# Value products of two attentions and a state-space mixer: values as the stationary operand, output by feature

## The chip, the cores and the metric

One core of one Trainium2 chip runs the whole kernel. The metric is device time in microseconds (us) of one execution; lower is better. The engines are TensorE (PE in the profile; PEld is its loading of the stationary operand), VectorE (DVE), ScalarE (ACT), GpSimd (POOL) and SyncE (SP, which issues the large loads).

## What is computed

One layer of a hybrid encoder, in float32: 256 tokens behind 16 meta tokens (272 in all), width 2048. The normed input is projected with `w_in`; four mixers of 512 features each work on the projection; their outputs are joined, projected with `w_out`, and a gated feed-forward block follows. Three mixers matter here. FoX and DSA are attentions of eight heads of 64 features; FoX with forget gates and a causal mask, DSA with keys chosen by an index score:

```python
s = jnp.where(key_pos[None, :] <= qpos[:, None], s, -jnp.inf)      # FoX
p = jax.nn.softmax(s, axis=-1).astype(v.dtype)
return jnp.einsum('bhqk,bkhd->bqhd', p, v)
```

SSD is a state-space mixer, also eight heads of 64 features. The kernel computes it as one masked product over all earlier tokens, `y = sum over s of m[l, s] * xdt[s] + d * x`, where `m` holds the decays times the products of the two projections `b` and `c`, and `xdt` is the input times its step `dt`.

## The kernel before, in words

**Weights.** All weights stream once from memory as 1 MB tiles (128 partitions x 2048). Each half tile is split into two parts of a shorter type, `whi` on ACT (line 148) and `wlo` on DVE (line 154), with four buffers of each. `tile_matmuls` (line 186) then issues, for each 128x128 block, three matmuls: high weights with high activations (line 202), high with low (203), low with high (204). In the projection these move 258 or 272 columns of tokens; the weights are stationary.

**Order.** The mixers are generators. After each half tile of weights (24 matmuls) `step(2)` (line 165) advances up to two of them to their next `yield`. So a mixer's work lies between half tiles of the projection. The instructions' final order on each engine is made by the framework's planner, which keeps dependences and goes by its own estimate of durations; on the chip each engine then runs its queue strictly in that order.

**Attention** (line 493, used by DSA and FoX) works on two tiles of 128 queries, `qt` 1 with 144 keys and `qt` 2 with 272. Scores come by query (lines 505 and 508), the maximum on DVE (513), the exponentials on ACT with their sum `st` (516). DVE then takes the reciprocal of the sums (518) and copies the meta tokens' part into `sm` (520). PE turns `sm` (522) and the eight heads' scores (531) to get the probabilities by key, copied by ACT to `p0` (524) and `pt` (533). For the values, `pt[:, h, :]` is stationary (128 keys x 128 queries) and the 64 columns of `v` of that head move (539); the meta tokens of all heads are one product of `p0` with a block-diagonal `blk` of 512 columns (541). The output `po` is by query; DVE multiplies it with the reciprocals into `o` (543); PE turns `o` back by feature with four transposes (547); ACT and DVE take its high and low parts `mh` and `ml` (549, 550), which `w_out` needs by feature. A float32 matmul shows as two records in the trace (two passes), a transpose as one.

**SSD** (line 672) keeps decays times products in `e1` (8 heads x 256 queries) and `e2` (8 x 128). `e1` is loaded by a DMA from POOL's queue (line 690) into the buffer that FoX's bias held, then DVE (699), ACT (700) and DVE (728) work on it. For `qt` 0, 1, 2 (2, 128 and 128 tokens) the values are formed as in the attention: `e1`, `e2` stationary, 64 columns of `xdt` moving (738, 741), the meta tokens' `e0` with `blk` of 512 columns (742), a copy on ACT (744), four transposes (748), and on DVE the skip term (750), four instructions per tile, into `yt`. The gate, the norm and the parts for `w_out` follow (757 to 769).

**Output projection.** For each group of four feature tiles of `w_out` the mixers come in the order DSA, pool, FoX, SSD; `drain(name)` first issues what is left of a mixer.

Of the kernel before, what the change touches and what calls it, by code (L numbers as in the profile page):

```python
# [12 lines left out]
P = 128  # L13
# [8 lines left out]
H = 8  # L22
# [15 lines left out]
# token tiles of all tokens (the meta tokens, then two of 128) and of the tokens whose mixed value is used  # L38
# [3 lines left out]
# per-partition columns  # L42
# [7 lines left out]
# constants: the unit matrix, its upper triangle, and rows that matmuls spread over the partitions  # L50
# [3 lines left out]
# groups of four feature tiles of w_in, by first column of the reference's order  # L54
# [15 lines left out]
# rows of w_out by the order in which the mixers end: dsa, fox, ssd, pool  # L70
# [9 lines left out]
def hybrid_layer(ctx: ExitStack, tc, t):  # L80
# [57 lines left out]
    def split_hi(i, half, n, pool=None):  # L138
        """The first parts of half a weight tile, in n pieces; gives the steps to the second parts."""
        load(i)  # L140
        hi = (pool or wpool).tile([P, 1024], F32R, tag="whi", bufs=4, name="whi")
        lo = (pool or wpool).tile([P, 1024], F32R, tag="wlo", bufs=4, name="wlo")
        halves[i, half] = (hi, lo)
        steps = []
        for q in range(n):
            c = slice(1024 * q // n, 1024 * (q + 1) // n)
            src = raws[i][:, 1024 * half + c.start:1024 * half + c.stop]
            act(hi[:, c], src, AF.Copy)  # L148
            steps.append((lo[:, c], src, hi[:, c].bitcast(F32)))
        return iter(steps)  # L150
# [35 lines left out]
    def tile_matmuls(accs, hi_lo, kts, n, feat, first, last, sub=None):  # L186
        """accs[f] += W tile.T @ activations; feat: weights stationary."""
        i = state["next"]
        state["next"] += 1
        for half in range(2):  # L190
            if (i, half) not in halves:
                split(i, half)
        load(i + 1)
        load(i + 2)
        def pair(f, half, kk):
            hi, lo = halves[i, half]
            k = 2 * half + kk
            xh, xl = hi_lo(kts[k])
            c = slice(kk * 512 + f * P, kk * 512 + (f + 1) * P)
            st = first and k == 0  # L200
            en = last and k == 3
            mm(accs[f][:, :n], hi[:, c], xh, start=st, stop=False)  # L202
            mm(accs[f][:, :n], hi[:, c], xl, start=False, stop=False)  # L203
            mm(accs[f][:, :n], lo[:, c], xh, start=False, stop=en)  # L204

        for part in range(2):
            if (i + 1, part) not in halves:
                split(i + 1, part)
            if last:
                # feature tile by feature tile, so that they end one after the other  # L210
                for f in (2 * part, 2 * part + 1):
                    for k in range(4):
                        pair(f, k // 2, k % 2)
            else:
                # the last feature tile's bank may still be read when a group begins
                late = first and part == 0 and i > 0
                for f, kk in sorted(((f, kk) for f in range(4) for kk in range(2)),
                                    key=lambda c: (c[0] == 3, c[1], c[0]) if late else (c[1], c[0])):
                    pair(f, part, kk)
            step(STEPS)  # L220
        for half in range(2):
            del halves[i, half]

# [1 line left out]
    def rstd_columns(small, sq, scale, segs, ps, meanwhile=None):  # L225
        """sq: lists of [128, tokens] whose sum over partitions and entries is the sum of squares."""
# [17 lines left out]
    def rsqrt(v, s, y, z, meanwhile=None):  # L244
        """y = v ** -0.5: a square root, a reciprocal and a step of Newton's method."""
# [11 lines left out]
    def rstd_rows(small, sq, scale, segs, out_rows):  # L257
        """The same by token along the free axis, on every partition."""
# [13 lines left out]
    # ================= input, mixers =================  # L272
# [19 lines left out]
    def root_table():  # L292
        """Loads the table of the square root before an argument waits for it."""
        pin(act(root, ones[:, 0:1], AF.Sqrt))
# [3 lines left out]
    def keep_warm(n):  # L298
        """Keeps TensorE's clock up while it waits."""
        ps = mix_ps()  # L300
        for _ in range(n):
            mm(ps[:, 0:P], ones, ones, start=True, stop=True)
# [82 lines left out]
    def small_values():  # L385
# [29 lines left out]
        # x: softplus; val: dt * -exp(a_log) and log_sigmoid  # L415
# [35 lines left out]
        # by head: the last two meta tokens' forget gates for FoX, the meta tokens' sums and dt for SSD  # L451
# [31 lines left out]
    def repeat(src, n, name):  # L483
        """The meta tokens once for each head, along the free axis."""
# [8 lines left out]
    def attention(name, q, k, v, blk, bias):  # L493
        """q, k by feature, v by token; bias(tile): the biases per head and the tile for the scores."""
        mh, ml = mixed_out(name)
        for qt, nk in ((1, 144), (2, 272)):
# [21 lines left out]
            V.reciprocal(st[:, 2, :], st[:, 1, :])  # L518
            sm = M.tile([P, P], F32, tag="p0", bufs=2, name="sm")
# [6 lines left out]
            for kt in range(1, qt + 1):  # L526
# [8 lines left out]
                pts.append(pt)  # L535
            po = mix_ps()
            for h in range(H):
                for j, pt in enumerate(pts):
                    mm(po[:, HD * h:HD * h + HD], pt[:, h, :], v[:, 1 + j, HD * h:HD * h + HD],
                       start=(h == 0 and j == 0), stop=False, skip_group_check=True)  # L540
            mm(po, p0, blk, start=False, stop=True, skip_group_check=True)
            o = M.tile([P, H, HD], F32, tag="o", bufs=2, name="o")
            V.tensor_tensor(o, po.rearrange("p (h d) -> p h d", d=HD), bcast(st[:, 2, :], [[1, H], [0, HD]]), ALU.mult)
            yield
            ps = mix_ps()
            for f in range(4):
                nc.tensor.transpose(ps[:, f * P:(f + 1) * P], o[:, 2 * f:2 * f + 2, :], ident)
            pv = ps.rearrange("p (a b) -> p a b", b=P)
# [3 lines left out]
        # the last two meta tokens, all heads at once: row 32 * pair + 2 * head in pair + token  # L552
# [119 lines left out]
    def ssd():  # L672
# [24 lines left out]
        # decays, from the sums of dt * a up to each token; later tokens' are masked with the scores  # L697
# [35 lines left out]
        for qt in (0, 1, 2):  # L733
            c0, n = SEGQ[qt]
            py = mix_ps()
            for h in range(H if qt else 0):
                hs = slice(HD * h, HD * h + HD)
                mm(py[:, hs], e1[:, h, (qt - 1) * P:qt * P], xdt[:, 1, hs], start=(h == 0), stop=False,
                   skip_group_check=True)
                if qt == 2:  # L740
                    mm(py[:, hs], e2[:, h, :], xdt[:, 2, hs], start=False, stop=False, skip_group_check=True)
            mm(py[0:n, :], e0[:, c0:c0 + n], blk, start=(qt == 0), stop=True, skip_group_check=True)
            y = M.tile([P, 512], F32, tag="o", bufs=2, name="y")
            act(y[0:n, :], py[0:n, :], AF.Copy)
            yield
            ps = mix_ps()
            for f in range(4):
                nc.tensor.transpose(ps[:, f * P:f * P + n], y[0:n, f * P:(f + 1) * P], ident[0:n, 0:n])
            for f in range(4):
                V.scalar_tensor_tensor(yt[:, f, c0:c0 + n], xs[:, f, L - LQ + c0:L - LQ + c0 + n], col(C_DSKIP + f),  # L750
                                       ps[:, f * P:f * P + n], op0=ALU.mult, op1=ALU.add)
            yield
# [111 lines left out]
    # ================= w_out, residual =================  # L864
# [15 lines left out]
    for f4 in range(4):  # L880
        accs = [acc() for _ in range(4)]
        if f4 == 3:
            # the table of the square root is loaded before the sum of squares waits for it
# [24 lines left out]
    # half a weight tile is split where the statistics wait  # L908
# [6 lines left out]
    # ================= FFN =================  # L915
# [9 lines left out]
    def turned(src, i, k0, ps):  # L925
        """Four feature tiles of 128 tokens, by token."""
# [7 lines left out]
    # half of the mixed values are turned while TensorE waits  # L934
# [17 lines left out]
    # new_x runs ahead of new_h: the addition on GpSimd lies between them  # L952
# [21 lines left out]
    def ffn_stats(gate):  # L974
# [9 lines left out]
        # in the columns that the finished gate tiles leave free  # L984
# [6 lines left out]
    def residual():  # L991
        # the second half of the features: added by token
# [64 lines left out]
    # ================= down projection =================  # L1057
# [121 lines left out]
```

## Time and profile before

| | before |
|---|---|
| timed runs, median (3 runs) | 1167.97 us (1167.88 to 1169.7) |
| profiled execution, from its first to its last instruction (span) | 1166.8 us |
| PE busy | 1143.9 us, 98% |
| PEld busy | 1075.9 us, 92% |
| DVE busy | 717.6 us, 62% |
| ACT busy | 539.4 us, 46% |
| POOL busy | 56.7 us, 5% |
| mean granted TensorE clock | 0.996 of full speed |

The profile is one execution of its own; of it only the span is recorded, not a time measured from outside. The span is 1.2 us under the median of the timed runs, which also hold what lies ahead of the first and behind the last instruction. Matmuls overlap in the pipeline, so the busy share of PE says only that it nearly always has something in work; the spacing from one start to the next is what a matmul costs.

### The profile page before, as it was taken

What the parts mean: (1) busy time and instruction counts of PE and PEld (TensorE: products, weight loads), DVE (VectorE), ACT (ScalarE), POOL (GpSimd) and SP (SyncE); (2) the same over time, 40 slices, a digit from 0 to 9 for tenths busy, and PEclk for the clock granted to TensorE, in tenths of its full rate; (3) what the DMA queues carried; (4) which work ended last, traced back from release to release, by engine and by line L of the source; (5) the groups of instructions that cost most, each with busy time, mean ns of one, the idle gap of its engine ahead of it and who ended that gap; (6) DMA issues with size and microseconds to landing.
All of it is one profiled execution on the core that took longest, in us unless ns stands there. A gap on an engine that the chain in (4) does not pass through costs nothing.

```text
span 1166.8 us, 19957 instructions
## 1 busy us (share of the span) xinstructions
PE 1143.9 (98%) x8349; PEld 1075.9 (92%) x8349; DVE 717.6 (62%) x1130; ACT 539.4 (46%) x768; POOL 56.7 (5%) x64
## 2 busy tenths in 40 slices
PE   7999999999999999999999999999999999999997
PEld 7999999998999999999999999999999888888885
DVE  8885675766765786565566556555655655544564
ACT  6434353563444555554444444444444444444452
POOL 6000010000000330000000000000000000000000
PEclk9999999999999999999999999999999999999999
DMA  7634444424555354555554555554555555555542
GB/s 269 213 146 145 165 168 161 151 98 168 182 181 186 144 213 165 199 180 187 187 188 171 202 186 181 181 181 181 181 183 183 195 195 183 180 187 196 193 182 72
DMA packets 32762, 207.34 MB, mean 178 GB/s; under 512 B 3712, under 2 KB 4896, under 8 KB 9376
## 3 DMA queue, kind: packets, MB, share of 16 engines
q1 hardware_dynamic: 30528, 198.80, 47.3%
q0 software_dynamic: 1568, 6.48, 1.8%
q8 instruction: 65, 1.06, 0.3%
q10 hardware_dynamic: 576, 0.79, 0.2%
q14 instruction: 25, 0.20, 0.1%
HBM read 203.93 MB, written 2.12 MB: 177 GB/s over the span
## 4 chain that ended last, share of the span: by engine, by line
PE 62%; DVE 1%; ACT 1%; POOL 1%; issue 0%; DVEq 0%; POOLq 0%; ACTq 0%
PE mx L203 7%; PE mx L202 7%; PE mx L204 7%; PE acc L203 7%; PE acc L204 7%; PE acc L202 7%; PE acc L1068 4%; PE acc L1069 4%; PE acc L1067 4%; PE mx L1069 3%; PE mx L1068 3%; PE mx L1067 3%; POOL ssum L981 1%; ACT whi L148 0%; DVE yo L1097 0%
## 5 line engine op out<-in xcount | busy, mean ns | idle before, releaser
L154 DVE TENSOR_TENSOR wlo<-raw,whi 128x1024 fp32r<-128x1024 f32 (+2 forms) x373 | 454.1, 1222 | 340.5 <-ACT whi L148 340.3
L148 ACT ACTIVATE whi<-raw 128x1024 fp32r<-128x1024 f32 (+2 forms) x373 | 387.0, 1046 | 485.3 <-PE acc L203 231.4
L203 PE MATMUL acc<-hl,whi 128*128 128x258 f32 x704 | 199.2, 283 | 1.0 <-DVE hl L949 0.9
L204 PE MATMUL acc<-hh,wlo 128*128 128x258 f32 x704 | 199.1, 283 | 0.0
L203 PE MATMUL mx<-hl,whi 128*128 128x256 f32 x704 | 198.6, 282 | 0.0
L202 PE MATMUL mx<-hh,whi 128*128 128x256 f32 x704 | 198.5, 282 | 0.0
L202 PE MATMUL acc<-hh,whi 128*128 128x258 f32 x704 | 198.2, 283 | 0.2 <-ACT hh L948 0.2
L204 PE MATMUL mx<-hh,wlo 128*128 128x256 f32 x704 | 197.9, 281 | 0.0
L202 PE MATMUL acc<-xh,whi 128*128 128x272 f32 (+1 forms) x576 | 173.5, 302 | 0.9 <-ACT whi L148 0.9
L204 PE MATMUL acc<-xh,wlo 128*128 128x272 f32 (+1 forms) x576 | 165.8, 291 | 5.7 <-DVE wlo L154 5.7
L203 PE MATMUL acc<-xl,whi 128*128 128x272 f32 (+1 forms) x576 | 166.2, 289 | 0.0
L203 PEld LDWEIGHTS acc<-hl,whi 128*128 128x128 f32 x704 | 133.3, 189 | 1.8 <-DVE hl L949 1.6
L203 PEld LDWEIGHTS mx<-hl,whi 128*128 128x128 f32 x704 | 133.1, 189 | 0.0
L204 PEld LDWEIGHTS mx<-hh,wlo 128*128 128x128 f32 x704 | 133.0, 189 | 0.0
L202 PEld LDWEIGHTS acc<-hh,whi 128*128 128x128 f32 x704 | 132.5, 189 | 0.4 <-ACT hh L948 0.4
L204 PEld LDWEIGHTS acc<-hh,wlo 128*128 128x128 f32 x704 | 132.8, 189 | 0.0
L202 PEld LDWEIGHTS mx<-hh,whi 128*128 128x128 f32 x704 | 132.7, 188 | 0.0
L202 PEld LDWEIGHTS acc<-xh,whi 128*128 128x128 f32 x576 | 110.4, 192 | 8.2 <-issue 5.8
L204 PEld LDWEIGHTS acc<-xh,wlo 128*128 128x128 f32 x576 | 109.4, 191 | 6.7 <-DVE wlo L154 6.3
L203 PEld LDWEIGHTS acc<-xl,whi 128*128 128x128 f32 x576 | 110.5, 192 | 1.8 <-issue 1.7
L1069 PE MATMUL acc<-wlo,yh 128*128 128x512 f32 x176 | 69.6, 396 | 0.0
L1068 PE MATMUL acc<-whi,yl 128*128 128x512 f32 x176 | 69.6, 396 | 0.0
(381 smaller groups left out, 1529.6 us busy)
## 6 DMA issues: line engine op xcount, KB each, us to landing
raw<-w_gate SPq DMA_DIRECT2D x44, 1024.0 KB, 4.8
raw<-w_up SPq DMA_DIRECT2D x44, 1024.0 KB, 4.8
raw<-w_down SPq DMA_DIRECT2D x44, 1024.0 KB, 4.8
raw<-w_in SPq DMA_DIRECT2D x32, 1024.0 KB, 4.8
raw<-w_out SPq DMA_DIRECT2D x16, 1024.0 KB, 4.8
raw<-w_in SPq DMA_DIRECT2D x6, 512.0 KB, 7.9
xT<-xT POOLq DMA_DIRECT2D x1, 2064.0 KB, 12.0
xr<-xT SPq DMA_DIRECT2D x4, 272.0 KB, 7.4
```

Of the source, the lines that this page charges most:

```text
L148: act(hi[:, c], src, AF.Copy)
L154: V.tensor_tensor(lo, src, hi, ALU.subtract)
L202: mm(accs[f][:, :n], hi[:, c], xh, start=st, stop=False)
L203: mm(accs[f][:, :n], hi[:, c], xl, start=False, stop=False)
L204: mm(accs[f][:, :n], lo[:, c], xh, start=False, stop=en)
L981: pin((G if k % 2 else V).tensor_tensor(ssum, ssum, sq, ALU.add))
L1067: mm(o, yh, hi[:, c], start=(k == 0), stop=False)
L1068: mm(o, yl, hi[:, c], start=False, stop=False)
L1069: mm(o, yh, lo[:, c], start=False, stop=(k == FT - 1))
```

## The change

The stationary operand of the value products becomes `v` (or `xdt`) of one head, 128 keys x 64 features, and the probabilities move, 128 queries (in SSD 256 or 128). The output then has 64 features of a head on 64 partitions, and the two heads of a pair take the lower and the upper 64 of the array's columns and of the output's partitions. `blk` becomes stationary in four blocks of 128 columns, with `p0` (128 columns) or `e0` (258) moving. Nothing has to be turned back, so the transposes, the tile `o` and SSD's ACT copy go. The reciprocals now lie along the wrong axis for the output, so the scores are scaled before they are turned: eight DVE instructions per query tile, on 128x144 or 128x272 elements. SSD's three tiles become four feature tiles with all 258 tokens each. Comments and docstrings are taken out as well, which changes no instruction.

```diff
@@ -516,6 +516,8 @@ attention
                 act(s[:, h, :], s[:, h, :], AF.Exp, bias=st[:, 0, h:h + 1], accum_out=st[:, 1, h:h + 1])
             yield
             V.reciprocal(st[:, 2, :], st[:, 1, :])
+            for h in range(H):
+                V.tensor_scalar(s[:, h, :], s[:, h, :], st[:, 2, h:h + 1], None, op0=ALU.mult)
             sm = M.tile([P, P], F32, tag="p0", bufs=2, name="sm")
             V.tensor_copy(sm.rearrange("p (h k) -> p h k", k=16), s[:, :, 0:16])
             ps = mix_ps()
@@ -533,23 +535,21 @@ attention
             po = mix_ps()
-            for h in range(H):
-                for j, pt in enumerate(pts):
-                    mm(po[:, HD * h:HD * h + HD], pt[:, h, :], v[:, 1 + j, HD * h:HD * h + HD],
-                       start=(h == 0 and j == 0), stop=False, skip_group_check=True)
-            mm(po, p0, blk, start=False, stop=True, skip_group_check=True)
-            o = M.tile([P, H, HD], F32, tag="o", bufs=2, name="o")
-            V.tensor_tensor(o, po.rearrange("p (h d) -> p h d", d=HD), bcast(st[:, 2, :], [[1, H], [0, HD]]), ALU.mult)
-            yield
-            ps = mix_ps()
             for f in range(4):
-                nc.tensor.transpose(ps[:, f * P:(f + 1) * P], o[:, 2 * f:2 * f + 2, :], ident)
-            pv = ps.rearrange("p (a b) -> p a b", b=P)
+                mm(po[:, f * P:(f + 1) * P], blk[:, f * P:(f + 1) * P], p0, start=(f == 0), stop=False,
+                   skip_group_check=True)
+            for j, pt in enumerate(pts):
+                for h in range(H):
+                    f, e = h // 2, HD * (h % 2)
+                    mm(po[e:e + HD, f * P:(f + 1) * P], v[:, 1 + j, HD * h:HD * h + HD], pt[:, h, :],
+                       start=False, stop=(j == qt - 1), skip_group_check=True)
+            pv = po.rearrange("p (a b) -> p a b", b=P)
@@ -730,25 +730,17 @@ ssd
         yt = q4(w=LQ, name="yt")
-        for qt in (0, 1, 2):
-            c0, n = SEGQ[qt]
-            py = mix_ps()
-            for h in range(H if qt else 0):
-                hs = slice(HD * h, HD * h + HD)
-                mm(py[:, hs], e1[:, h, (qt - 1) * P:qt * P], xdt[:, 1, hs], start=(h == 0), stop=False,
-                   skip_group_check=True)
-                if qt == 2:
-                    mm(py[:, hs], e2[:, h, :], xdt[:, 2, hs], start=False, stop=False, skip_group_check=True)
-            mm(py[0:n, :], e0[:, c0:c0 + n], blk, start=(qt == 0), stop=True, skip_group_check=True)
-            y = M.tile([P, 512], F32, tag="o", bufs=2, name="y")
-            act(y[0:n, :], py[0:n, :], AF.Copy)
-            yield
+
+        for f in range(4):
             ps = mix_ps()
-            for f in range(4):
-                nc.tensor.transpose(ps[:, f * P:f * P + n], y[0:n, f * P:(f + 1) * P], ident[0:n, 0:n])
-            for f in range(4):
-                V.scalar_tensor_tensor(yt[:, f, c0:c0 + n], xs[:, f, L - LQ + c0:L - LQ + c0 + n], col(C_DSKIP + f),
-                                       ps[:, f * P:f * P + n], op0=ALU.mult, op1=ALU.add)
+            mm(ps[:, 0:LQ], blk[:, f * P:(f + 1) * P], e0, start=True, stop=False, skip_group_check=True)
+            for i, e, c in ((1, e1, 2), (2, e2, 2 + P)):
+                for h in (2 * f, 2 * f + 1):
+                    r = HD * (h % 2)
+                    mm(ps[r:r + HD, c:LQ], xdt[:, i, HD * h:HD * h + HD], e[:, h, :], start=False, stop=(i == 2),
+                       skip_group_check=True)
+            V.scalar_tensor_tensor(yt[:, f, :], xs[:, f, L - LQ:L], col(C_DSKIP + f), ps[:, 0:LQ],
+                                   op0=ALU.mult, op1=ALU.add)
             yield
```

## Rows read from the trace of the kernel before

**Rows 1.** The page: busy time and share of PE; granted clock in 40 slices.

```profile
PE 1143.9 (98%) x8349; PEld 1075.9 (92%) x8349; DVE 717.6 (62%) x1130; ACT 539.4 (46%) x768; POOL 56.7 (5%) x64
...
PEclk9999999999999999999999999999999999999999
```

**Rows 2.** Windows: length, busy us (instructions) by engine, clock, DMA share, GB/s.

```profile
120.00:180.00 60.00, 59.48 (x470) 55.82 (x470) 41.04 (x78) 27.38 (x48) 5.62 (x8) 1.00 0.45 159
```

**Rows 3.** PE timeline, DSA's first query tile: start, us, line, output<-operands, records.

```profile
120.25 1.89 PE L539 MATMUL mx<-vp,pt 128*128 128x64 f32 x16
...
123.02 0.28 PE L203 MATMUL acc<-xl,whi 128*128 128x258 f32 x1
123.14 0.28 PE L204 MATMUL acc<-xh,wlo 128*128 128x258 f32 x1
...
125.77 0.60 PE L547 MATMUL mx<-cst,o 128*128 128x128 f32 x4
...
126.33 0.28 PE L203 MATMUL acc<-xl,whi 128*128 128x258 f32 x1
```

**Rows 4.** PE timeline, DSA's second query tile.

```profile
162.23 3.68 PE L539 MATMUL mx<-vp,pt 128*128 128x64 f32 x32
...
166.79 0.29 PE L203 MATMUL acc<-xl,whi 128*128 128x272 f32 x1
```

**Rows 5.** PE timeline, SSD's meta tokens, and its second tile of 128.

```profile
269.09 1.02 PE L742 MATMUL mx<-blkssd,e 128*2 128x512 f32 x2
...
270.27 0.29 PE L203 MATMUL acc<-xl,whi 128*128 128x272 f32 x1
...
290.88 0.43 PE L738 MATMUL mx<-xdt,e 128*128 128x64 f32 x2
...
295.53 0.28 PE L203 MATMUL acc<-mldsa,whi 128*128 128x258 f32 x1
```

**Rows 6.** PE timeline around L713: two float32 matmuls of 64 stationary columns, side by side.

```profile
245.58 0.28 PE L204 MATMUL acc<-xh,wlo 128*128 128x258 f32 x1
...
246.61 0.28 PE L203 MATMUL acc<-xl,whi 128*128 128x258 f32 x1
```

**Rows 7.** Line 580: records, ns min/median/max, first and last start, form.

```profile
L580 PE MATMUL mx<-p0m,vp x16: 192/193/213, 179.9 to 180.3; 16*64 16x2 f32 x16
```

**Rows 8.** PE timeline, float32 matmuls of 128 stationary columns.

```profile
255.03 0.60 PE L721 MATMUL mx<-bc 128*128 128x256 f32 x2
255.46 0.38 PE L722 MATMUL mx<-bc 128*128 128x128 f32 x2
255.68 0.60 PE L531 MATMUL mx<-cst,fb 128*128 128x128 f32 x4
```

**Rows 9.** DVE groups by form, 20 to 420 us: busy us, mean ns, idle before.

```profile
L543 DVE TENSOR_TENSOR o<-mx,st 128x512 f32<-128x512 f32 x4 | 2.7, 686 | 0.5 <-PE mx L541 0.4
...
L788 DVE TENSOR_SCALAR fb<-fb,cum 128x272 f32<-128x272 f32 x8 | 2.3, 354 | 1.0 <-DMA fb<-drow 1.0
L750 DVE SCALAR_TENSOR_TENSOR yt<-xs,cols,mx 128x128 f32<-128x128 f32 x8 | 2.2, 341 | 1.9 <-PE mx L748 1.9
...
L783 DVE TENSOR_SCALAR fb<-fb,cum 128x144 f32<-128x144 f32 x8 | 1.7, 286 | 0.0
```

**Rows 10.** Waits of PE, whole span: total us, times, longest.

```profile
PE mx L522 <- DVE sm L520: 0.5, 1, 0.5
```

**Rows 11.** DVE timeline, FoX's second tile into SSD; idle before and its releaser in brackets.

```profile
265.73 1.23 DVE L154 TENSOR_TENSOR wlo<-raw,whi 128x1024 fp32r<-128x1024 f32 x1 [1.29 <-ACT whi L148]
272.27 2.19 DVE L699 TENSOR_SCALAR e<-e,cum 128x256 f32<-128x256 f32 x8 [5.32 <-DMA e<-drow]
274.38 0.68 DVE L543 TENSOR_TENSOR o<-mx,st 128x512 f32<-128x512 f32 x1
```

**Rows 12.** PE timeline, the same stretch.

```profile
273.04 0.29 PE L204 MATMUL acc<-xh,wlo 128*128 128x272 f32 x1
275.12 0.66 PE L547 MATMUL mx<-cst,o 128*128 128x128 f32 x4 [1.79 <-DVE o L543]
275.71 0.50 PE L748 MATMUL mx<-cst,y 2*128 2x2 f32 x4
276.14 0.60 PE L202 MATMUL acc<-xh,whi 128*128 128x272 f32 x1
```

**Rows 13.** Windows, the stretch after that wait; columns as in rows 2.

```profile
275.80:279.30 3.50, 3.50 (x18) 3.48 (x19) 3.05 (x7) 2.05 (x3) 0.00 (x0) 0.51 0.00 0
```

## The prediction

> **What bounds the kernel now.** I read the page first: PE is busy 98% of the span and holds its full clock in nearly every slice [rows 1]. The reader should not stop there, since overlapping matmuls make PE look busy at any speed; so next come the windows of the stretch in which the mixers run. Between 120 and 180 us PE has work in 59.5 of 60 us at clock 1.00, DVE in 41.0 and ACT in 27.4 [rows 2]. PE never waits there for long; the other two have a third or more of their time free, DMA more than half. So what PE is spared in this stretch should be spared in the end, and what DVE gains in work is free as long as nobody waits for it. The third view, the timeline of PE, prices the work: ordinary weight matmuls start every 0.12 us (123.02, 123.14 in [rows 3]; 0.125 with 272 columns), and a group of mixer work costs what it pushes the next weight matmul back.
>
> **What goes on PE.** DSA's first query tile: the 16 value records start at 120.25; with the two of `blk` behind them they push the weight stream so that line 203 starts at 123.02. The first weight matmul behind such a group shows an early start and a long duration, so I take the second and go back one step of 0.12: the group held PE until 122.90, 2.65 us. The four transposes: 125.77 to 126.33 less 0.12, 0.44 us [rows 3]. Second tile, 32 records and `blk`: 162.23 to 166.79 less 0.125, 4.43 us [rows 4], and again 0.44. Sum for DSA 7.96 us; FoX issues the same shapes, so 15.9 for both.
>
> SSD: the meta tokens' tile, 269.09 to 270.27 less 0.125, is 1.05 us for 512 columns that serve two tokens [rows 5]; its four small transposes 0.43 (275.71 to 276.14, [rows 12]). The first tile of 128 has the 18 records of DSA's first tile, 2.65, and 0.44 of transposes. The second: 290.88 to 295.53 less 0.12, 4.53 [rows 5], and 0.44. Sum 9.5. Together 25.5 us of PE go.
>
> **What comes on PE.** A float32 record with 128 stationary and 128 moving columns costs 0.11 us (two in 255.46 to 255.68), one with 256 moving 0.215 (two in 255.03 to 255.46) [rows 8]. Before, a value record took 0.115 us (3.68 for 32 [rows 4]), though only 64 columns moved: there the load of 128 stationary columns sets the pace. The new `blk` part is four matmuls, eight records, 0.88 us per query tile.
>
> The value records now have 64 stationary columns, one head in each half of the array. Do two heads run at once? Line 580 has that very form, two heads alternating, with 2 columns moving: its 16 records start within 0.4 us, so 7 steps of a pair take about 0.057 us each [rows 7]. Line 713, with 258 columns moving, is nearer in size: two matmuls, four records, push the stream from 245.58 to 246.61; less two steps of 0.12 this is 0.79 us [rows 6]. Four records one after the other would need 4 x 0.215 = 0.86 by [rows 8] before any switching; two pairs need 0.43 and leave 0.36 for what entering and leaving the split array costs. I take side by side: per pair of records 0.112 us with 128 columns moving, and 0.36 per group for the switch. The lower end of a pair is the 0.11 of the moving columns; the upper, if the loads of 64 columns aren't hidden, 0.11 + 0.057 (line 580, where there is nothing but load). I take the lower end, since in the ordinary stream loads are hidden.
>
> Per attention: first tile 0.88 + 8 pairs x 0.112 + 0.36 = 2.14; second 0.88 + 16 x 0.112 + 0.36 = 3.03; both attentions 10.3. SSD, four times: `blk` with 258 columns 2 x 0.215, two pairs with 256 columns 0.43, two with 128 0.22, switch 0.36, together 1.44; 5.8 in all. PE gets 16.1 us and loses 25.5: **9.4 us less**.
>
> **The other engines.** DVE gets 8 scalings per tile: the nearest rows are eight in-place instructions of the same kind and size, 1.7 us for 144 columns and 2.3 for 272 [rows 9]: 4.0 per attention, 8.0 in all. It loses four `o` of 0.69, 2.7 us, and SSD's twelve skip terms become four (of twelve, eight took 2.2 us [rows 9]); a saving there is taken as nothing. Net 5 us over a stretch of some 180 us, where DVE is a third idle. ACT loses three copies of 512 columns; it isn't the bound, nothing.
>
> What stands behind the scalings in DVE's queue? `sm`, for which line 522 on PE waits, and the next split `wlo`. The split is covered: in [rows 11] DVE runs none between 266.96 and the stall of PE at 273, five of those microseconds merely waiting, and the weight matmuls run on from their four buffers. Should that cover go, the scalings cost PE up to their own 2.3 us per tile. Line 522 is less well covered: it already waited once for `sm`, 0.5 us [rows 10]. There the planner decides: it sees the scalings and should put the transposes that much later between weight matmuls. I take nothing for it; the upper end is a rival below. No DMA is issued anew; `e1`'s load on POOL's queue waits for FoX's last read of the scores, which comes 1.7 + 2.3 us later for FoX's scalings and some 3.7 us earlier for the PE work saved ahead (2.8 in DSA, 0.95 in FoX's first tile).
>
> **The one stall of the stretch.** FoX's second `o` stood on DVE behind line 699, which had waited 5.3 us for the DMA of `e1` [rows 11]. PE waited with line 547 from 273.04 + 0.125 to 275.12, some 1.96 us, and then ran at clock 0.51, the lower of its two levels (1.2 of 2.4 GHz), for 3.5 us [rows 12, 13], of which half is lost, 1.7 us. Line 547 goes. But the DMA isn't any faster, and the new SSD products need `e1` too, with 1.5 us less of PE work ahead of them than the old meta-token tile gave. What is late next is line 728's product, so I let the same loss of about 3.7 us reappear there and book no gain.
>
> **Sum.** The profiled span of 1166.8 would become 1157.4; with the 1.2 us that the median lies above it, 1168.0 - 9.4 = **1158.6 us**.
>
> **Rivals.** (a) The stall goes for good, since no PE instruction now sits between DVE's queue and `e1` except SSD's own, and the planner has weight matmuls to fill in: 9.4 + 3.7 = 13.1, **1154.9**. For it: PE's only long wait in the stretch was that one. Against: the same DMA.
>
> (b) The loads of the 64-column operands aren't hidden: 64 pairs (48 in the attentions, 16 in SSD) x 0.057 = 3.7 us back, a gain of 5.7, **1162.3**. For it: line 580's step is all load, and line 713's 0.36 us over its columns may hold some of it. Against: in the ordinary stream a load of the next block lies under the running matmul. The Trainium skill ("TensorE: Matmul & The Clock Gate", Part 3, The mechanism) has the rule that such a load overlaps a running matmul only if it uses other rows of the array; both heads use all 128 rows, so by it this rival holds. The ordinary stream, which uses all rows too and starts every 0.12 us [rows 3], speaks against the rule as stated.
>
> (c) The stall comes back larger, because PE reaches SSD (or the pool mixer behind it) some 9 us sooner than the DVE and DMA chains do; one more stall like [rows 12], 3.7 us: **1162.3**.
>
> (d) The heads don't run side by side for wide operands: 48 + 16 pairs become serial, 56 x 0.112 with 128 columns and 8 x 0.215 with 256, 8.0 us back, a gain of 1.4: **1166.6**, no change that counts.
>
> (e) Slower: line 522 keeps its place in PE's queue and waits for the scalings in all four query tiles. The price is the scalings, 8.0 us, and behind each wait a fall of the clock as in [rows 13], 4 x 1.7 = 6.8: 14.8 - 9.4 = +5.4, **1173.4**. It decides from about 2.4 us of loss per tile on. For it: that line runs close behind `sm` already. Against: the planner orders by readiness, and one wait of 0.5 us in four tiles is all there is now.
>
> **How the numbers follow.** Forecast 0.45, (a) 0.16, (b) 0.13, (c) 0.11, (d) 0.05, (e) 0.10. The range from 1154.0 to 1164.0 holds the forecast, (a), (b) and (c), with a microsecond each for the unknown switch cost (0.36 x 8 = 2.9 us in all). A measurement of this kernel can tell 0.2%, 2.3 us, from no change: faster by more has the first four cases less a little, 0.84; same 0.07; slower 0.09.
>
> **What would show it.** The value records of the two heads should start in pairs, some 0.01 us apart, a pair every 0.11 to 0.12 us; at 0.16 it is (b), at 0.22 (d). A first query tile's group should push the weight stream by about 2.1 us, a second by 3.0, each of SSD's four by 1.4. The waits of PE should show line 522 with under 1 us in all; more is (e). Look between FoX's end and SSD's first products for a wait on `e1`, and at the granted clock behind it. The prediction is wrong if the records pair and the time still doesn't fall by some 6 us: then the wait list of PE must hold the difference.

## The result, and the profile after

| | before | after |
|---|---|---|
| median of the timed runs | 1168.84 us (1167.88 to 1170.42, 4 runs) | 1160.87 us (1160.43 to 1161.67, 4 runs) |
| ratio to before | | 0.9938, 95% interval 0.9921 to 0.9955 |
| span of the profiled execution | 1166.8 us | 1159.3 us |
| mixers' stretch in it | 292.6 us | 283.9 us |
| rest in it | 726.7 us | 728.2 us |

The changed kernel is 8.0 us faster; 9.4 were forecast. The forecast time was 1158.6 us, 2.3 below the measured one; 0.9 of that is the kernel before, whose median is 1168.84 with a fourth run where the forecast started from 1168.0. The ratio in the table is the recorded one with its interval; the quotient of the two medians is 0.9932. The profiled execution was also timed from outside this time, 1161.08 us, 1.8 over its span.

Two stretches are used below. The mixers' stretch runs from the first score product (line 505) to line 255 behind `w_out`; in the changed kernel these two rows of PE's timeline bound it, 386.70 - 102.79 = 283.91:

```profile
102.79 0.39 PE L505 MATMUL mx<-kp,udq 64*128 64x144 f32 x2
...
386.70 0.55 PE L255 MATMUL mx<-cst,rs 2*128 2x2 f32 x3 [0.65 <-DVE rs L252]
```

The rest runs from the sums of squares of the feed-forward block's norm (line 231, at 431.11 us) to the end. The mixers gave 8.7 us; the rest, in which nothing was changed, took 1.5 more. What lies ahead of the mixers was 0.3 shorter, so the spans differ by 7.5.

The page's busy times and clock, which answer to [rows 1]:

```profile
PE 1136.5 (98%) x8331; PEld 1068.6 (92%) x8331; DVE 721.6 (62%) x1150; ACT 541.6 (47%) x767; POOL 56.0 (5%) x64
...
PEclk9999999999999999999999999999999999999998
```

PE is as full as before, with 7.4 us less in work. The timeline of PE shows why, at DSA's first query tile [rows 3]; line 541 is now `blk`, line 546 the values:

```profile
120.02 0.28 PE L204 MATMUL acc<-xh,wlo 128*128 128x258 f32 x1
120.14 1.05 PE L541 MATMUL mx<-p,blkdsa 128*128 128x128 f32 x8
121.12 1.09 PE L546 MATMUL mx<-pt,vp 128*64 128x128 f32 x16
122.15 0.39 PE L202 MATMUL acc<-xh,whi 128*128 128x258 f32 x1
122.37 0.29 PE L203 MATMUL acc<-xl,whi 128*128 128x258 f32 x1
```

Sixteen value records with 128 moving columns take 1.09 us, where sixteen with 64 took 1.89. The group holds PE from 120.14 to 122.37 less one step of 0.12, 2.11 us, and no transposes follow. The second tile's 32 records take 1.97 us, where 32 took 3.68 [rows 4], and its group holds PE for 2.99:

```profile
157.82 1.05 PE L541 MATMUL mx<-p,blkdsa 128*128 128x128 f32 x8
158.81 1.97 PE L546 MATMUL mx<-pt,vp 128*64 128x128 f32 x32
160.71 0.39 PE L202 MATMUL acc<-xh,whi 128*128 128x272 f32 x1
160.93 0.29 PE L203 MATMUL acc<-xl,whi 128*128 128x272 f32 x1
```

An SSD feature tile:

```profile
282.30 0.60 PE L736 MATMUL mx<-e,blkssd 128*128 128x258 f32 x2
282.83 0.87 PE L740 MATMUL mx<-e,xdt 128*64 128x256 f32 x8
283.86 0.29 PE L203 MATMUL acc<-xl,whi 128*128 128x272 f32 x1
```

That is 1.44 us. Some waits of PE over the whole span (waited for, then us in total, times, longest):

```profile
PE acc L231 <- POOL ssum L973: 2.3, 1, 2.3
PE mx L573 <- DVE s L570: 2.0, 1, 2.0
...
PE mx L524 <- DVE sm L522: 0.8, 3, 0.3
```

The wait for FoX's `o` [rows 12] is gone with its transposes. In its place stands one at line 573, the transpose of DSA's scores of the last two meta tokens, 100 us earlier. Line 524 is the old 522 [rows 10]. Line 231's wait is in the kernel before too, of the same length, 2.3 us. The clock fell to the lower level (1.2 of 2.4 GHz) behind two of these waits; the windows, with columns as in [rows 2]:

```profile
173.40:176.90 3.50, 3.50 (x16) 3.50 (x17) 1.47 (x3) 1.87 (x4) 0.30 (x1) 0.51 0.63 211
432.80:436.30 3.50, 3.50 (x18) 3.32 (x16) 0.99 (x5) 0.06 (x1) 0.00 (x0) 0.51 0.51 215
```

The first is the fall of [rows 13] at another place. The second has no counterpart in the profile of before, where the window from 437 to 444 us, which holds the same wait and 3.9 us behind it, shows clock 1.00.

### The profile page after: what moved, and what is told of

The parts are those of the page before. It is cut to its first block, busy times and chain, and to the rows that moved or that the text cites. A ratio compares the mean times of both kernels' runs of the same rounds, so it can differ in the third digit from the quotient of the medians.

```text
span 1159.3 us, 19938 instructions
## 1 busy us (share of the span) xinstructions
PE 1136.5 (98%) x8331; PEld 1068.6 (92%) x8331; DVE 721.6 (62%) x1150; ACT 541.6 (47%) x767; POOL 56.0 (5%) x64
## 4 chain that ended last, share of the span: by engine, by line
PE 63%; DVE 1%; POOL 0%; ACT 0%; issue 0%; DVEq 0%; ACTq 0%; POOLq 0%
PE mx L203 7%; PE mx L202 7%; PE mx L204 7%; PE acc L204 7%; PE acc L203 7%; PE acc L202 7%; PE acc L1060 4%; PE acc L1061 4%; PE acc L1059 4%; PE mx L1061 3%; PE mx L1060 3%; PE mx L1059 3%; POOL ssum L973 0%; DVE yo L1089 0%; DVE yo L1103 0%
```

## The experiments

Each was profiled; times are medians of timed runs beside runs of the kernel before in the same session (1168.5 us for the first four, 1168.3 for the others). Single runs of one kernel lie up to 8 us apart (e2: 1162.7 to 1171.0), so the stretches in the profiles decide where a few microseconds are asked for. Each stretch is that of one profiled execution.

| | median (runs) | ratio to before, 95% interval | mixers' stretch | rest |
|---|---|---|---|---|
| e1_one_half | 1160.27 (4) | 0.9923 (0.9902 to 0.9944) | 283.6 | 729.5 |
| e2_attention_alone | 1165.18 (10) | 0.9972 (0.9954 to 0.9990) | 286.7 | 728.1 |
| e3_ssd_alone | 1165.01 (8) | 0.9965 (0.9954 to 0.9977) | 289.1 | 726.7 |
| e4_meta_later | 1159.52 (4) | 0.9913 (0.9888 to 0.9939) | 280.2 | 729.6 |
| e5_halves_apart | 1164.38 (5) | 0.9963 (0.9945 to 0.9981) | 286.7 | 728.2 |
| e6_norm_filled | 1155.90 (4) | 0.9891 (0.9875 to 0.9907) | 280.2 | 726.7 |
| e7_no_scaling | 1161.74 (1) | | 284.4 | 728.2 |
| e8_before_o_later | 1167.92 (1) | | 290.6 | 728.2 |

### Which half gains what: e2 and e3

```diff
e2: kernel before, attention() of the changed kernel, the loop behind `yt` in ssd() as before
e3: kernel before, attention() as before, the loop behind `yt` in ssd() of the changed kernel
```

> Edit: the kernel before with the changed attention; SSD as it was. Theory (PE's work sets the time): the attentions give 15.9 - 10.2 = 5.7 us of PE work, so about 1163 us, if the stalls cost what they do in the changed kernel; up to 3.7 us more or less where one comes or goes. Rival (the gain lies in SSD, whose chain ends last among the mixers): less than 2 us, 1167 or more.

> Edit: the kernel before with the changed SSD; the attention as it was. Theory: 9.5 - 5.8 = 3.7 us of PE work less, about 1165 us; the wait of PE for FoX's o stays, since line 547 stays. Rival (the gain lies in SSD's chain): 6 us or more less, 1163 or below.

The stretch fell by 6.0 us for the attention (5.7 expected) and by 3.6 for SSD (3.7). The timed medians, 3.3 and 3.5 us under before, don't separate the two. The waits differ: e3 keeps line 547's wait for `o`, 2.1 us, with the fall of the clock behind it (275.7 us). e2 has line 573's wait instead, longer than the changed kernel has it, and yet the clock stayed at the upper level behind it (a row of PE's timeline, then a window):

```profile
172.64 0.27 PE L573 MATMUL mx<-cst,s 128*16 128x128 f32 x1 [2.56 <-DVE s L570]
...
172.70:176.20 3.50, 3.50 (x39) 3.33 (x39) 1.52 (x3) 3.27 (x6) 0.29 (x1) 1.00 0.30 51
```

With the stalls of each kernel counted (3.7 us in before; 2.7 and 0.5 more at SSD's norm in e2; 4.0 and 0.3 more at an earlier `o` in e3), PE's work fell by an estimated 5.5 us in e2 and 4.2 in e3. That the gain lies mainly in SSD is excluded by the stretches.

### Do two heads run side by side: e1 and e5

```diff
 e1
-                for h in range(H):
+                for h in (0, 2, 4, 6, 1, 3, 5, 7):
                     f, e = h // 2, HD * (h % 2)
```

> Edit: the changed kernel, but in both attentions the value products take the heads in the order 0, 2, 4, 6, 1, 3, 5, 7, so that neighbours in PE's queue use the same half of the array; same instructions, same sizes, same data. Theory (two heads run side by side): each of the 24 pairs of records per attention becomes two records of 0.11 us; a first query tile's group goes from 2.1 to 3.0 us, a second from 3.0 to 4.8, the time rises by 5.4 us, to about 1166.3. Rival (the gain comes from the shorter loads of 64 columns and the missing transposes alone): no change, 1160.9 within 1 us, and the groups keep their size.

Neither was right. The groups of line 541 and 546 grew, but to 2.60 and 3.59 us, not to 3.0 and 4.8, and the time didn't rise. In the profile of e1:

```profile
121.33 1.05 PE L541 MATMUL mx<-p,blkdsa 128*128 128x128 f32 x8
122.31 1.58 PE L546 MATMUL mx<-pt,vp 128*64 128x128 f32 x16
123.82 0.39 PE L202 MATMUL acc<-xh,whi 128*128 128x258 f32 x1
```

Sixteen records take 1.58 us, less than 16 x 0.11 = 1.76. The records do not name their half, but their starts fall into two series of eight, 0.11 us apart within a series; the second series starts at 122.80, when three records of the first have not started. So PE, as I read it, let work of the free half past waiting work of the other, and the edit didn't part the halves. What is said of the queues under "Order", that each engine runs its queue strictly in that order, then does not hold between two halves of PE's array. The four groups together cost 2.2 us more; but line 573 now came 1.1 us too early instead of 2.0, and the clock didn't fall behind it, which gives back 0.9 + 1.7. The sum, -0.4, is what the stretch shows, -0.3. A cleaner edit, on a base without that wait (e4 below; only the added lines, shortened):

```diff
 e5
+            for e in (0, 1):
+                for f in ((0, 1, 2), (3,))[e]:
+                    mm(po[:, f * P:(f + 1) * P], blk[:, f * P:(f + 1) * P], p0, start=(f == 0), stop=False, ...)
+                for j, pt in enumerate(pts):
+                    for h in range(e, H, 2):
+                        mm(po[HD * e:HD * e + HD, ...], v[:, 1 + j, HD * h:HD * h + HD], pt[:, h, :], ...)
```

> Base: e4_meta_later, which has no long wait of PE among the mixers, so that more PE work should show in full. Edit: in both attentions three of the four blk products, then all heads of the lower half, then the fourth blk product (full width), then all heads of the upper half; the same instructions, but the two halves of the array can't have work at once. Theory (side by side): 24 pairs per attention become 48 single records of 0.11 us, and each query tile enters and leaves the split array once more, 0.36 us: a first tile's group 2.1 to 3.4, a second 3.0 to 5.1, together 6.8 us; the mixers' stretch (first score product to the norm behind w_out) goes from 280.2 to 287. Rival (shorter loads and missing transposes alone make the gain): only the switches, 1.4 us, 281.6.

The stretch rose from 280.2 to 286.7, by 6.5 us where 6.8 were expected, and the time from 1159.5 to 1164.4. The groups took 3.32 and 5.07 us (3.4 and 5.1 expected):

```profile
120.68 0.83 PE L542 MATMUL mx<-p,blkdsa 128*128 128x128 f32 x6
121.44 1.09 PE L547 MATMUL mx<-pt,vp 128*64 128x128 f32 x8
122.46 0.49 PE L542 MATMUL mx<-p,blkdsa 128*128 128x128 f32 x2
122.88 1.09 PE L547 MATMUL mx<-pt,vp 128*64 128x128 f32 x8
123.89 0.39 PE L202 MATMUL acc<-xh,whi 128*128 128x258 f32 x1
```

Eight records of one half take the 1.09 us that sixteen of both took. The same instructions with the same loads, but one half at a time, lose what the attention had gained; of the 6.5 us, 1.4 are the four added switches and the rest the heads one after the other. Two heads at once are the gain, not the short loads.

### Where the stall went: e4 and e8

```diff
 e4 (changed kernel, behind the scaling of the last two meta tokens' scores)
         yield
+        if name == "dsa":
+            yield
+            yield
         ps = mix_ps()
         nc.tensor.transpose(ps[0:16, 0:P], s0[:, 0:16], ident)
```

> Edit: the changed kernel with two more yields in DSA between the scaling of the last two meta tokens' scores and their transpose, so that the transpose stands 28 weight matmuls later in PE's queue; no instruction more or less. Theory (the loss that I had left at SSD's e1 has moved to DSA's end, where PE waits 2.0 us for these scores and then runs 3.4 us at half clock): both go, about 3.7 us, to 1157.2; PE has no wait over 1 us between 60 and 380 us. Rival (the chain on DVE and ACT is late as a whole, so the wait turns up at the next instruction that needs it): 1160.9 within 1 us, with a wait of some 2 us at another line.

The stretch went from 283.91 to 280.20, by the 3.7 us expected, and PE has no wait over 0.3 us left in it but one of 0.7 at its end, for the norm behind `w_out`. The timed median fell less, to 1159.5 (1157.2 expected), since the rest took 729.6: in this execution the clock stood at the lower level for 7 us behind line 231 instead of 3.5:

```profile
427.70:434.70 7.00, 7.00 (x34) 6.71 (x35) 1.92 (x7) 0.94 (x2) 0.00 (x0) 0.51 0.38 150
```

What held line 573 up in the changed kernel is seen on DVE:

```profile
162.88 2.26 DVE L780 TENSOR_SCALAR fb<-fb,cum 128x272 f32<-128x272 f32 x8 [1.70 <-DMA fb<-drow]
165.06 0.69 DVE L550 TENSOR_TENSOR mldsa<-mx,mhdsa 128x512 fp32r<-128x512 f32 x1
165.66 1.73 DVE L154 TENSOR_TENSOR wlo<-raw,whi 128x1024 fp32r<-128x1024 f32 x1
167.31 0.16 DVE L563 TENSOR_SCALAR s<-mx 128x16 f32<-128x16 f32 x1
...
171.50 0.23 DVE L570 TENSOR_SCALAR s<-s 128x16 f32<-128x16 f32 x1
```

The chain of the two meta tokens starts at line 563, behind FoX's bias (line 780, eight instructions that first waited for their DMA) and a split, and has a table load of 1.28 us on ACT in it. The scores were ready at 171.7; PE stood there from 169.7. In the kernel before PE came to the same transpose just behind its scores, which were ready at 176.5. The rows of before, then that of the changed kernel:

```profile
176.27 0.23 DVE L570 TENSOR_SCALAR s<-s 128x16 f32<-128x16 f32 x1
176.65 0.27 PE L573 MATMUL mx<-cst,s 128*16 128x128 f32 x1
...
171.88 0.27 PE L573 MATMUL mx<-cst,s 128*16 128x128 f32 x1 [1.97 <-DVE s L570]
```

PE came 6.9 us sooner, the scores only 4.8. PE's lead is not only work saved (2.9 us in DSA's two tiles): with the transposes of each query tile a `yield` went too, and so line 573 stands behind 1028 weight matmuls instead of 1056, 28 x 0.125 = 3.5 us. e4's two yields put it back behind 1056.

```diff
 e8 (kernel before, behind FoX's second o)
             yield
+            if name == "fox" and qt == 2:
+                yield
+                yield
             ps = mix_ps()
```

> Base: the kernel before. Edit: two more yields between FoX's second o and its transposes, so that these stand 48 weight matmuls later; no instruction more or less. My step (what is late next is e1, so the loss of 3.7 us reappears at SSD's first product with e1): the mixers' stretch stays at 292.6 within 1 us, with a wait of 1 to 2 us at SSD's first product. Rival (the wait was that of o alone): the wait and the fall of the clock go, 288.9.

The stretch was 290.6, between the two. PE no longer waited long for `o`, but the wait did turn up at SSD's first product with `e1`, which is line 741 in this kernel:

```profile
278.48 1.08 PE L741 MATMUL mx<-xdt,e 128*128 128x64 f32 x8 [1.20 <-DVE e L731]
```

Its 1.2 us came without a fall of the clock. So my step had the right successor and the wrong price: of 3.7 us, 2.0 went.

### What the scalings cost: e7

```diff
 e7 (on e4)
-            for h in range(H):
-                V.tensor_scalar(s[:, h, :], s[:, h, :], st[:, 2, h:h + 1], None, op0=ALU.mult)
```

> Base: e4_meta_later. Edit: without the eight scalings per query tile (the division of the attention's outputs by the sums is left out). Theory (the scalings are hidden, since the planner puts the transposes of the scores some 24 weight matmuls later): the mixers' stretch stays within 1 us of 280.2; at most the three waits for sm, 0.8 us, change. Rival (the scalings hold PE up, by up to their 8.0 us): 275 or less.

Both missed: without the scalings the stretch was 4.2 us longer. The waits for `sm` fell to 0.2 us, and DSA's transposes stood up to 26 weight matmuls earlier in PE's queue (behind 687 of them instead of 710, and 908 instead of 934). But PE met the stall on `e1` that I had forecast for the changed kernel itself:

```profile
267.15 0.29 PE L203 MATMUL acc<-xl,whi 128*128 128x272 f32 x1
270.69 0.76 PE L741 MATMUL mx<-e,xdt 128*64 128x256 f32 x6 [3.25 <-DVE e L729]
```

The clock fell behind it as well (272.3 to 275.7 us). PE was there only 0.8 us sooner than in e4, where this product started at 268.08; what came late was `e1`. Its DMA started at 254.6 us, in e4 at 255.1, but took 10.6 us instead of 6.9, and more weights came in beside it, 2.02 MB against 0.56. The rows are the queue of the weights during that load (packets, MB, share of the DMA engines' time) and the load itself (KB, us to landing), of e7, then of e4:

```profile
q1 hardware_dynamic: 272, 2.02, 48.4%
e<-drow POOLq DMA_DIRECT2D x1, 1024.0 KB, 10.6
...
q1 hardware_dynamic: 68, 0.56, 20.0%
e<-drow POOLq DMA_DIRECT2D x1, 1024.0 KB, 6.9
```

The ten profiles fall apart in the same way: with the scalings (the changed kernel, e1, e2, e4, e5, e6) `e1`'s load took 6.9 to 7.5 us beside 0.6 MB of weights, without them (before, e3, e7, e8) 9.6 to 10.6 beside 2.0 to 2.9 MB. e7 shows that the scalings make the difference; that it is the weights beside the load is a reading, since no run moves the weights alone. With the stall and the fall taken out (3.4 + 1.7 us), e7's stretch would be 279.3, 0.9 under e4's. By that estimate the scalings cost PE under 1 us of their 8.0, because the planner moved what waits for them; that they also make `e1`'s load 3.7 us shorter was luck.

### The fall of the clock in the rest: e6

```diff
 e6 (on e4, in ffn_stats)
+        for _ in range(10):
+            mm(gate[3][:, 272:400], ones, ones, start=True, stop=True, skip_group_check=True)
         y = rstd_columns(T, [[ssum]], 1.0 / D, SEGQ, gate[3][:, 264:272])
```

> Base: e4_meta_later. Edit: ahead of the sums of squares of the feed-forward block's norm, where PE waits 2.3 us for the last addition, ten products of ones into free columns of a finished bank. Theory (the wait of 2.3 us stands in the kernel before too, but in the profiles of the changed kernel the clock fell behind it for 3.4 or 6.8 us and in the profile of before it did not; so the rest of my missing microseconds is this fall, not the mixers): no fall, the part from those sums to the end takes 726.7 us as before instead of 728.2 to 729.6, and the time is 1.5 to 2.9 us under e4's in the profile. Rival (the fall has another cause, or comes at another place): the part stays at 728 to 730.

The rest took 726.69 us, as before the change, and the time fell to 1155.9, 3.6 us under e4 and 12.4 under the kernel before. Two windows of its profile hold the place of the wait and all that follows, both at clock 1.00 as rounded (at the very end, here the last 6.5 us, the clock is down in every version):

```profile
420.00:445.00 25.00, 24.91 (x210) 24.53 (x209) 18.67 (x38) 15.52 (x28) 5.80 (x5) 1.00 0.38 132
445.00:1155.50 710.50, 701.89 (x4861) 653.20 (x4859) 399.60 (x524) 314.86 (x390) 0.58 (x1) 1.00 0.52 182
```

Two of the nine profiles without the filling, before and e3, have no fall there either, so this one profile alone does not prove it; the timed runs speak for it, 1155.8 to 1157.3 in e6 against 1155.0 to 1160.7 in e4. This is the fastest version here: the change, with DSA's last transpose two steps later and the norm's wait filled.

## Why the prediction was right, and where it was off

**PE's work: right, term by term.** A first query tile was to take 2.14 us and took 2.11, a second 3.03 and 2.99, an SSD tile 1.44 and 1.44. e2 and e3, with their stalls counted, give the two sums alone within 0.5 us (5.5 for 5.7, 4.2 for 3.7). The switch of 0.36 us per group, read from line 713, held in all of them; e5, which adds one to each query tile, costs what it says.

**Side by side: right**, shown by e5. Rivals (b) and (d) are out. For (b) the records of the second tile suffice: 16 pairs in 1.97 us is 0.11 a pair after the tail of the last one, where unhidden loads wanted 0.17. By the Trainium skill's rule ("TensorE: Matmul & The Clock Gate", Part 3, The mechanism), a load overlaps a running matmul only on other rows; the trace disagrees, since here both heads use all 128 rows and their loads of 64 columns lie fully under the moving columns, a pair of records every 0.11 us. The same section of the Trainium skill also lets a load run ahead when it goes to the background weight buffer, which would fit; no row here shows where a load goes.

**The scalings: right to book nothing, for the reason given.** Rival (e) needed line 522 to keep its place; the planner put it behind 710 weight matmuls instead of 687. The waits grew from 0.5 to 0.8 us in all.

**The stall: the size came out, the place did not.** The step that failed is "what is late next is line 728's product, so I let the same loss of about 3.7 us reappear there", and its ground, "But the DMA isn't any faster". In the changed kernel PE waited nowhere for `e1`: its DMA started at 258.5 us instead of 262.3 and took 7.0 instead of 10.0, so DVE waited 1.2 us for it where it had waited 5.3 [rows 11]. The prediction let the start stay about where it was (4.0 us later for FoX's scalings, 3.7 sooner for PE's work) and had no term for the `yield` that went with each query tile's transposes: FoX's last read of the scores now stands behind 1584 weight matmuls instead of 1608, 3.0 us. The shorter load came with the scalings (e7). A loss of the same size, 2.0 us of wait and a fall of 3.5 us, stood at DSA's last transpose, which the prediction did not look at and which the missing yields had moved up as well. e4 removes it for 3.7 us. That the sum came out in the mixers (8.7 of 9.4) is thus luck as far as this term goes. Rival (a) was right that `e1` would hold PE up no longer; with DSA's stall gone too (e4) the mixers gave 12.4 us of its 13.1. Rival (c) was right that PE can come too soon for a chain on DVE, but at DSA's end and with one stall, not two. The remaining 0.7: 0.3 more wait at line 524, the rest unassigned.

**The missing 1.5 us** behind the mixers are the second fall of the clock, 3.5 us at half speed. The prediction took it for granted that unchanged stretches keep their time. Line 231's wait is as long in every version but e6; whether the clock falls behind it, and for how long, differed between profiles, and the rest follows it: 726.7 us without a fall (before, e3, e6), 728.1 to 728.2 with 3.5 us of it (the changed kernel, e2, e5, e7, e8), 729.5 to 729.6 with 7 (e1, e4). e8, which has the old products, has the fall too, so it does not need the change; how often it comes in the timed runs of each kernel is not shown.

## What to carry to other kernels

Where a product has few moving columns and 128 stationary ones, the load sets the pace (here 0.115 us a record with 64 moving columns, 0.11 with 128); swapping the operands puts the long side on the moving one, and if the other side is 64, two products run at once in the two halves of the array. Price it from the trace as whole groups, by how far they push the stream behind them, with the switch included. When a stall vanishes, list every instruction on the bound engine that hangs on the other engines' chains, not only the next one, and count how far the edit moves each in that engine's queue. And before calling a small rest a loss of the change, compare unchanged stretches and fill the waits behind which the clock may fall.

## What the runs showed of the hardware that was not expected

The two halves of the array are fed past each other: in e1, eight records of one half and then eight of the other took 1.58 us, less than one after the other (1.76), the second series starting after five records of the first.

Going into and out of the split array costs 0.35 to 0.36 us per group in all kernels here, as much as three pairs of records; by that estimate a group with less than about four pairs would not repay it.

The length of a wait did not settle whether the clock falls behind it. A wait of 2.0 us was followed by 3.5 us at the lower clock in the changed kernel (line 573), one of 2.6 at the same place in e2 by none, one of 1.1 there in e1 and one of 1.2 at line 741 in e8 by none, and the same 2.3 us at line 231 by none, 3.5 or 7.

`e1`'s load of 1 MB took 6.9 to 7.5 us in some kernels and 9.6 to 10.6 in others, and eight scalings on DVE per query tile decided which (e4 and e7).
